# Attention per query block: denominators and values in four 32-column groups, the reciprocal on VectorE, and the first tile's q/k/v between the matmuls of the last layer-0 MLP

## The chip, the cores and the metric

The kernel runs on all eight NeuronCores of one Trainium2 chip, one launch, each core on its own half of one sample. The metric is the device time of the slowest core in microseconds (us). An execution can fall in a slower state, in which the cores of one die get a lower TensorE clock (one of e1_lnexp: 1792.11 us, four cores at 0.816 to 0.822, the other four at 0.983 to 0.991); every run lists the clock and span of each core, and only runs of the fast state are compared here. Engine names in the profile: PE is TensorE (PEld its weight loads), DVE is VectorE, ACT is ScalarE, POOL is GpSimd.

## The reference, cut to what matters

Two layers over 4 samples of 4096 tokens of width 1024, in front of each a modulated RMSNorm, behind each mixer a squared-ReLU MLP. Layer 0 mixes by pooling, layer 1 by windowed attention, which is where the change lies:

```python
# window_attention: 16 heads of 64, 2 key/value heads, blocks of 128 queries
q = rope_2d(q, ang) * qscale;  k = rope_2d(k, ang)
s_win  = ...   # keys of the previous, own and next block, |i-j| <= 128
s_ctx  = ...   # 256 context keys
p = softmax(concat([s_win, s_ctx, s_sink], -1))     # a sink logit per head
o = p_win @ v_win + p_ctx @ v_ctx
y = o.reshape(B, L, 1024) @ w_o
```

For one query block of 128 there are five key blocks of 128: previous, next, own, and two of context. The kernel keeps probabilities transposed (keys on partitions), so a softmax denominator is a matmul with a matrix of ones, and division follows the values.

## The kernel before

Every operation is recorded with the tiles that it reads and writes. A list scheduler then orders each engine's instructions with a cost per instruction that is written in the code, and the order is fixed from then on. All matmuls go through one helper and have one line in the profile (L378; L387 after the change), so groups are told apart by their tiles. A matmul whose weights have 64 columns writes 64 output partitions, and two of them on different halves run side by side: in the trace of before the two of a pair start within 40 ns, and the next pair follows 0.216 us after them.

```python
SB = [P.bk(0, 2), P.bk(2, 2)]            # scores: two pairs of PSUM banks
OB, DB = P.bk(4), P.bk(5)                # values, denominators; banks 6, 7 serve everything else

def emit_s(p, i):                        # scores of one key block and half (8 heads), Exp on ScalarE, mask
    ...
    P.act(pt.rearrange("p a b -> p (a b)"), sb, AF.Exp, scale=0.125)
    ...

def emit_pv(p):                          # p: query block and half
    qb, hf = pairs[p]
    for v in range(2):                   # the sink starts the denominator
        P.mm(DB[64 * v:64 * v + 64, :]..., ONES, ESKR[...], start=True, stop=False)
    for i in (2, 3, 4, 0, 1):
        for v in range(2):
            P.mm(DB[64 * v:64 * v + 64, :], ONES, pt_of(p, i)[:, v, :], start=False, stop=(i == 1))
    for i in (2, 3, 4, 0, 1):
        kb, _ = kbs_of(qb)[i]
        for v in range(2):
            P.mm(OB[64 * v:64 * v + 64, :], VA[:, kb, 64 * v:64 * v + 64], pt_of(p, i)[:, v, :], start=(i == 2), stop=(i == 1))

def emit_o(p):
    ...
    P.act(DN, DB, AF.Ln)                 # 1/x as exp(-ln x), twice over 128x512
    P.act(DN, DN, AF.Exp, scale=-1.0)
    P.tt(QT[...][...], OB..., DN..., ALU.mult)
```

Between scores and values the loop over 80 steps fills in other TensorE work: projections of tiles 1 to 3 (512 tokens each), the output projections, and the first matmuls of the layer-1 MLP. The projections of the 384-column halo and context tile (tile 4) and of tile 0 come before the loop, after the last layer-0 MLP:

```python
spread(mlp_2(gb), wkv_dma + n4 + n0, 4)          # the last MLP half; norms of tiles 4 and 0 between its matmuls
...
run_all(l1_proj(4))
...
spread(l1_proj(0), l1_norm(1, RS[0]), 1)         # k, v, q of tile 0: matmul, then rope on VectorE and GpSimd
```

The softmax here doesn't subtract the row's maximum and nothing guards it: scores larger than these inputs give would overflow.

## Time and profile before

| | before |
|---|---|
| time, median of the first 3 runs | 1549.28 us (1548.54 to 1549.91) |
| spans of the eight cores, profiled run | 1538.8 to 1544.6 us, clock 0.984 to 0.989 |
| TensorE busy | 94% of the span |
| TensorE idle in attention (777 to 1082 us) | 30 us of 305 |

The first part of the page of before (busy us of each engine, share of the span, instructions) and the first line of its chain of waits (who held the chain that ended last):

```profile
PE 1453.5 (94%) x8116; PEld 703.0 (46%) x8116; DVE 604.2 (39%) x1003; ACT 593.9 (38%) x860; POOL 303.0 (20%) x369
...
PE 88%; DVE 3%; DMA 3%; issue 3%; ACT 2%; POOL 1%; SPq 0%; DVEq 0%; ACTq 0%; POOLq 0%
```

TensorE is the bottleneck. What it does less of can count in full; what other engines do counts only where TensorE waits. The windows view of before, over attention (columns: stretch, its length, busy us and instructions of PE, PEld, DVE, ACT and POOL, granted clock, DMA share, GB/s):

```profile
777.00:1082.00 305.00, 274.75 (x1727) 110.77 (x1726) 170.25 (x253) 216.78 (x262) 161.36 (x148) 0.96 0.12 21
```

Here TensorE is idle for 30 us and its clock is cut to 0.96 on average. The clock takes two values in the clock records of before, 1 and 0.5, so 0.96 means 2 x 0.04 x 305, some 24 us at half clock. TensorE's waits of before in attention (who waited for whom, us in total, times, longest):

```profile
PE ps L378 <- POOL qt_115 L405: 6.0, 1, 6.0
PE ps L378 <- DVE tbe_126 L419: 3.5, 1, 3.5
PE ps L378 <- POOL pt_113 L424: 3.4, 1, 3.4
```

The two longest are the start: the first scores wait for tile 0's q, which comes out of a chain of VectorE and GpSimd work. The timeline of TensorE before, one half block (start, length, operation, count):

```profile
1046.04 0.41 PE L378 MATMUL ps<-eskr_50,ones_47 128*64 128x512 bf16 x2
1046.28 0.38 PE L378 MATMUL ps<-pt_108,ones_47 128*64 128x512 bf16 x2
1046.50 0.38 PE L378 MATMUL ps<-pt_109,ones_47 128*64 128x512 bf16 x2
...
1048.22 0.38 PE L378 MATMUL ps<-pt_107,va_105 128*64 128x512 bf16 x2
1048.54 0.61 PE L378 MATMUL ps<-qt_118,kt_104 64*128 64x512 bf16 x4
```

Lengths overlap (0.38 us, while the next pair starts after 0.22 us); the start-to-start distance is what counts. A pair takes one slot of 0.216 us. A half block has eleven slots (one for the sink, five for denominators, five for values), 2.50 us from its first matmul to the next scores.

### The profile page before, as it was taken

Reading aid. Unit: us, or ns where it says so; the run is one execution under the profiler, and the core shown is the slowest. Engines: PE = TensorE matmul, PEld = TensorE weight load, DVE = VectorE, ACT = ScalarE, POOL = GpSimd, SP = SyncE. Lnnn points to the kernel's source line nnn. Section 1 sums busy time; section 2 is a strip of 40 time slices with the busy share of each in tenths; the row PEclk is TensorE's granted clock in tenths of the full one; section 3 lists DMA queues with packets and bytes.
Section 4 is the critical chain, followed back from the end, with each engine's and each line's share of the span. In section 5 each row is a group of like instructions: output and inputs, shape, how many; then the busy total and the mean of one; then the engine's idle time right before and its main releaser. Section 6 shows DMA issues by size and latency. Waiting matters only on the chain.

```text
span 1544.6 us, 22776 instructions; the slowest of 8 cores (1538.8 to 1544.6 us)
## 1 busy us (share of the span) xinstructions
PE 1453.5 (94%) x8116; PEld 703.0 (46%) x8116; DVE 604.2 (39%) x1003; ACT 593.9 (38%) x860; POOL 303.0 (20%) x369
## 2 busy tenths in 40 slices
PE   1699899999999999999978989989999999999996
PEld 0344345555555555555533433333444444444442
DVE  0177874442221444222188664433343221553013
ACT  2464363335110333331047858877234221432001
POOL 2025400101100001000137664444000000000000
PEclk9999999999999999999989989999999999999998
DMA  9554715455653454653340012001244444654432
GB/s 191 147 123 79 127 28 96 83 102 90 113 106 66 85 96 83 112 107 67 63 69 8 8 28 42 0 1 28 42 82 70 78 72 75 129 123 83 71 66 109
DMA packets 38958, 121.69 MB, mean 79 GB/s; under 512 B 3904, under 2 KB 4288, under 8 KB 38464
## 3 DMA queue, kind: packets, MB, share of 16 engines
q0 software_dynamic: 28656, 100.48, 37.8%
q1 hardware_dynamic: 10192, 19.76, 4.0%
q8 instruction: 67, 1.10, 0.3%
q14 instruction: 43, 0.35, 0.1%
HBM read 212.30 MB, written 8.39 MB: 143 GB/s over the span
## 4 chain that ended last, share of the span: by engine, by line
PE 88%; DVE 3%; DMA 3%; issue 3%; ACT 2%; POOL 1%; SPq 0%; DVEq 0%; ACTq 0%; POOLq 0%
PE ps L378 88%; DMA xm_55<-xT 2%; DMA ring_59<-ada_r 0%; DVE xm_55 L415 0%; DMA ring_58<-ada_r 0%; SPq L438 0%; DVE tmp_64 L405 0%; ACT xb_68 L388 0%; DVE tmp_65 L405 0%; ACT rs_63 L388 0%; DVE tb_122 L419 0%; ACT pt_112 L388 0%; DVE tb_121 L405 0%; POOL h_134 L412 0%; DVE tb_123 L405 0%
## 5 line engine op out<-in xcount | busy, mean ns | idle before, releaser
L415 DVE SCALAR_TENSOR_TENSOR xm_55<-ps,mod_44,xm_55 128x512 f32<-128x512 f32 (+2 forms) x136 | 97.4, 719 | 338.4 <-PE ps L378 337.9
L388 ACT ACTIVATE tmp_64<-ps 128x512 f32<-128x512 f32 (+2 forms) x155 | 84.0, 542 | 228.3 <-PE ps L378 176.2
L388 ACT ACTIVATE tmp_65<-ps 128x512 f32<-128x512 f32 (+2 forms) x155 | 84.0, 542 | 141.5 <-PE ps L378 77.0
L388 ACT ACTIVATE sqf_169<-xm_55 128x1024 bf16<-128x1024 f32 x16 | 16.6, 1051 | 158.6 <-DVE xm_55 L415 156.6
L378 PE MATMUL ps<-xb_68,win_67 128*128 128x512 bf16 (+1 forms) x192 | 50.6, 424 | 10.2 <-ACT xb_68 L388 9.5
L378 PE MATMUL ps<-h_0_98,ring_61 128*128 128x408 bf16 (+3 forms) x336 | 58.9, 335 | 0.0
L378 PE MATMUL ps<-h_0_98,ring_58 128*128 128x384 bf16 (+3 forms) x336 | 58.9, 335 | 0.0
L388 ACT ACTIVATE rs_63<-ps,epsv_51 128x512 f32<-128x512 f32 (+3 forms) x16 | 10.6, 664 | 123.6 <-PE ps L378 123.5
L405 DVE TENSOR_TENSOR tmp_64<-xm_55,rs_63 128x512 f32<-128x512 f32 (+2 forms) x44 | 37.4, 850 | 43.7 <-ACT rs_63 L388 35.8
L378 PE MATMUL ps<-h_0_98,ring_60 128*128 128x416 bf16 (+3 forms) x288 | 50.5, 335 | 0.0
L378 PE MATMUL ps<-h_0_98,ring_59 128*128 128x416 bf16 (+3 forms) x288 | 50.4, 334 | 0.0
L378 PE MATMUL ps<-h_0_98,ring_57 128*128 128x416 bf16 (+3 forms) x288 | 50.4, 334 | 0.0
L438 POOL DMA_DIRECT2D ring_61<-w_r x27 | 14.3, 531 | 162.5 <-PE ps L378 162.0
L405 DVE TENSOR_TENSOR hid_100<-tmp_64 128x416 bf16<-128x416 f32 (+3 forms) x48 | 27.9, 581 | 43.1 <-ACT tmp_64 L388 43.1
L438 POOL DMA_DIRECT2D ring_59<-w_r x27 | 14.4, 533 | 151.7 <-PE ps L378 144.5
L378 PEld LDWEIGHTS ps<-h_0_98,ring_61 128*128 128x128 bf16 x336 | 32.5, 97 | 25.1 <-issue 0.6
L405 DVE TENSOR_TENSOR hid_99<-tmp_64 128x416 bf16<-128x416 f32 (+3 forms) x48 | 27.9, 581 | 40.8 <-ACT tmp_64 L388 40.6
L378 PEld LDWEIGHTS ps<-h_0_98,ring_58 128*128 128x128 bf16 x336 | 32.5, 98 | 25.0 <-issue 0.8
L405 DVE TENSOR_TENSOR hid_99<-tmp_65 128x416 bf16<-128x416 f32 (+3 forms) x48 | 27.9, 581 | 38.2 <-ACT tmp_65 L388 38.2
L405 DVE TENSOR_TENSOR hid_100<-tmp_65 128x416 bf16<-128x416 f32 (+3 forms) x48 | 27.9, 581 | 36.8 <-ACT tmp_65 L388 36.8
L378 PE MATMUL ps<-hid_99,ring_61 128*128 128x416 bf16 (+3 forms) x240 | 42.1, 335 | 0.0
L388 ACT ACTIVATE h_134<-xm_55 128x1024 bf16<-128x1024 f32 (+1 forms) x12 | 15.9, 1344 | 67.9 <-PE ps L378 67.9
(769 smaller groups left out, 3083.1 us busy)
## 6 DMA issues: line engine op xcount, KB each, us to landing
ring_61<-w_r POOLq DMA_DIRECT2D x27, 512.0 KB, 5.2
ring_59<-w_r POOLq DMA_DIRECT2D x27, 512.0 KB, 5.7
ring_57<-w_r POOLq DMA_DIRECT2D x25, 512.0 KB, 5.2
ring_58<-w_r POOLq DMA_DIRECT2D x25, 512.0 KB, 5.1
ring_60<-w_r POOLq DMA_DIRECT2D x24, 512.0 KB, 5.1
outT<-xm_55 SPq DMA_DIRECT2D x16, 512.0 KB, 3.3
xm_55<-xT SPq DMA_DIRECT2D x6, 1024.0 KB, 8.7
ring_58<-ada_r POOLq DMA_DIRECT2D x12, 512.0 KB, 6.0
```

What stands on the lines that cost most here:

```text
L378: return self.S.op("pe", lambda e: e.matmul(out, lhsT, rhs, start=start, stop=stop), reads=[lhsT, rhs], writes=[out], cost=max(30.0 if hal ...
L388: return self.S.op("act", lambda e: e.activation(out, in_, func, bias=bias, scale=scale), reads=[in_, scale, bias], writes=[out], cost=175 ...
L405: return self.S.op(eng, lambda e: e.tensor_tensor(out, in0, in1, op), reads=[in0, in1], writes=[out], cost=self.ew_cost(eng, "tt", out, [i ...
L415: return self.S.op("dve", lambda e: e.scalar_tensor_tensor(out, in0, scalar, in1, op0, op1), reads=[in0, in1, scalar], writes=[out], cost= ...
L438: return self.S.op(q, lambda e: e.dma_start(out=out, in_=in_), reads=[in_], writes=[out], chan="dma:" + slot, inc=16, extra_deps=dep, cost ...
```

## The change

The intent has three parts.

1. The 32 denominator-and-value passes, one per half block, become 16, one per query block, with four weight groups of 32 columns side by side. Denominators need only 6 slots a block instead of 12; values stay at 10.
2. The reciprocal of the denominators is taken on VectorE, in place of Ln and Exp on ScalarE.
3. Tile 4's k and v and tile 0's k, v and q are made between the matmuls of the last layer-0 MLP, with the squares and statistics of tiles 1 and 2.

The two banks 4 and 5 now go round: denominators, first value half, second value half, and so on, so the second value half writes the bank from which the reciprocal reads. The diff, cut to its core:

```diff
+    def recip(self, out, in_):
+        return self.S.op("dve", lambda e: e.reciprocal(out, in_), reads=[in_], writes=[out], cost=160.0 + 1.04 * self.n_of(out))
...
-    OB, DB = P.bk(4), P.bk(5)
+    AB = [P.bk(4), P.bk(5)]
...
-    def emit_pv(p): ...
-    def emit_o(p): ...
+    def emit_pv(qb):
+        groups = [(hf, v) for hf in range(2) for v in range(2)]
+        q0 = (qb % 4) * 128
+        db = rot("ab", AB)
+        with S.one():
+            for g in range(4):
+                P.mm(db[32 * g:32 * g + 32, :]..., ONES, ESKR[...], start=True, stop=False)
+            for i in range(5):
+                for g, (hf, v) in enumerate(groups):
+                    P.mm(db[32 * g:32 * g + 32, :], ONES, pt_of(qb, i, hf)[:, v, :], start=False, stop=(i == 4))
+        with S.first(20):
+            P.recip(DN, db)
+        for dh in range(2):
+            ob = rot("ab", AB)
+            with S.one():
+                for i in range(5):
+                    kb, _ = kbs_of(qb)[i]
+                    for g, (hf, v) in enumerate(groups):
+                        P.mm(ob[32 * g:32 * g + 32, :], VA[:, kb, 64 * v + 32 * dh:64 * v + 32 * dh + 32], pt_of(qb, i, hf)[:, v, :],
+                             start=(i == 0), stop=(i == 4))
+            with S.first(20):
+                P.tt(QT[qb // 4][:, 4 * dh:4 * dh + 4, q0:q0 + 128], ob..., DN..., ALU.mult)
...
-    spread(mlp_2(gb), wkv_dma + n4 + n0, 4)
+    sides_gb = n4 + [early_dma] + kv_pieces(4) + n0 + kv_pieces(0)     # q of tile 0 rides on the weight stream
+    for _ in mlp_2(gb):
+        step += 1
+        if sides_gb:
+            sides_gb.pop(0)()
+        if step % 6 == 0 and step >= 18:
+            ...
+            for t in (1, 2):
+                stat_chunk(t, step // 6 - 3)
...                                        # SBUF places, 12 probability tiles, filler 1500 instead of 2500 ns a step,
...                                        # output-projection rows permuted to match
```

More of the change, by code (lines that the diff above doesn't have):

```diff
@@ L161, in f, with first @@
             self.hold, self.boost = None, 0
+        return f()
+    def first(self, boost):
+        @contextmanager
+        def f():
+            self.boost = boost
+            yield
+            self.boost = 0
         return f()
@@ L378, in mm @@
         return self.S.op("pe", lambda e: e.matmul(out, lhsT, rhs, start=start, stop=stop), reads=[lhsT, rhs], writes=[out],
-                         cost=max(30.0 if half else 62.0, (n / 2.4 + 2.5) * (0.5 if half and n > 64 else 1.0)),
+                         cost=max(30.0 if half else 62.0, (n / 2.4 + 2.5) * (min(rows, cols) / 128.0 if n > 64 else 1.0)),
                          mode=(rows, cols), join=join)
@@ L526, in build @@
     ONESM = const("onesm", [128], BF16)
-    ONES = const("ones", [64], BF16)
+    ONES = const("ones", [32], BF16)
     CTF = const("ctf", [16], F32)
@@ L560, in build @@
     ada_n = [0]
+    extra = {}
     def ada_mm(slot, c, MB):
@@ L604, in w_take @@
             pass
+        nxt = ST.items[ST.pos][0]
+        if nxt[0] in extra:
+            extra[nxt[0]](*nxt[1:])
         return ST.take(key)
@@ L611, in build, with plan_mlp @@
             ST0.add(("ada", 0, r, c), d_ada[0, r, c])
-    def plan_mlp(l, g, rounds1, rounds2):
+    def plan_mlp(l, g, rounds1, rounds2, q0={}):
         ext1 = [("ada", l_, r_, c) for l_, r_ in rounds1 for c in range(4)]
@@ L622, in plan_mlp @@
             ST.add(("w2", l, g, j), d_w2[l, j // 2, j % 2])
+            if j in q0:
+                ST.add(("wq0", q0[j]), d_wq[q0[j]])
             if ext2 and j >= 1:
@@ L628, in build @@
     plan_mlp(0, 0, [(0, 5), (1, 1)], [(1, 0), (1, 2)])
-    plan_mlp(0, 1, [(1, 3), (1, 4)], [(1, 5)])
+    plan_mlp(0, 1, [(1, 3), (1, 4)], [(1, 5)], {11: 0, 12: 1, 13: 2, 14: 3})
     for i in range(4):
@@ L652, in norm_sq, with rms_of @@
             o += n
+    def rms_of(bk, N, rs):
+        P.act(rs[:, 0:N], bk[:, 0:N], AF.Ln, bias=EPSV)
+        P.act(rs[:, 0:N], rs[:, 0:N], AF.Exp, scale=-0.5)
     def norm_stat(sq, N, rs):
@@ L657, in norm_stat @@
             P.mm(bk[:, 0:N], ONESM, sq[:, c, 0:N], start=(c == 0), stop=(c == NCH - 1))
-        P.act(rs[:, 0:N], bk[:, 0:N], AF.Ln, bias=EPSV)
-        P.act(rs[:, 0:N], rs[:, 0:N], AF.Exp, scale=-0.5)
+        rms_of(bk, N, rs)
     def norm_apply(tile, rs, l, n, h, c, eng="act", tmps=None):
@@ L1032, in build @@
     DN = P.t("dn", E0 + 9728, [512], F32)
-    PT = [ft("pt", i * 2048, [2, 512], BF16) for i in range(8)]
-    QTO = (16384, 24576, 65536, 73728)
+    ROPE0 = P.t("ropee", E0 + 9728, [1024], BF16)
+    ROPE4 = P.t("ropee", E0 + 11776, [2, 128], BF16)
+    PT = [ft("pt", i * 2048, [2, 512], BF16) for i in range(12)]
+    QTO = (38912, 24576, 74752, 38912)
     QT = [ft("qt", o, [NCH, 512], BF16) for o in QTO]
-    WO0, WO17 = ft("wo", 32768, [1024], BF16), ft("wo", 81920, [7, 1024], BF16)
-    TBO = (34816, 36864, 38912, 40960, 43008)
+    WO0, WO17 = ft("wo", 32768, [1024], BF16), ft("wo", 82944, [7, 1024], BF16)
+    TBO = (34816, 36864, 66560, 68608, 55296)
     TB = [ft("tb", o, [512], F32) for o in TBO[0:4]]
-    TBE = [ft("tbe", i * 2048, [512], F32) for i in range(8)]
-    HB = [ft("h", o, [NCH * 512], BF16) for o in (45056, 57344)]
-    HH = {4: sqv(ft("h", 38912, [NCH * 384], BF16), 384), 0: sqv(HB[0], 512), 1: sqv(HB[1], 512), 2: sqv(HB[0], 512), 3: sqv(HB[1], 512)}
-    WKV = ft("wkv", 53248, [2, NCH, 128], BF16)
+    TB4 = [ft("tbk", 55296 + i * 512, [128], F32) for i in range(2)]
+    TBK = [ft("tbk", o, [512], F32) for o in (43008, 45056)]
+    HB = [ft("h", o, [NCH * 512], BF16) for o in (47104, 58368)]
+    HH = {4: sqv(ft("h", 47104, [NCH * 384], BF16), 384), 0: sqv(HB[0], 512), 1: sqv(HB[1], 512), 2: sqv(HB[0], 512), 3: sqv(HB[1], 512)}
+    WKV0, WKV1 = [ft("wkv", o, [2, NCH, 128], BF16) for o in (38912, 70656)]
     SHUF = [i ^ 16 for i in range(32)]
@@ L1059, in rope_dma, with rope, l1_kv @@
         k = rot("rope", [0, 1])
-        rope_of[t] = rope_slots[k]
-        P.dma("pool", rope_of[t], d_rope[t].rearrange("p a b -> p (a b)"), slot="rope%d" % k)
-    def l1_proj(t):
+        rope_of[t] = rope_slots[k].rearrange("p (a b) -> p a b", a=2)
+        P.dma("pool", rope_slots[k], d_rope[t].rearrange("p a b -> p (a b)"), slot="rope%d" % k)
+    def rope(t, ba, dst, n, tb, post=None):
+        rp = rope_of[t]
+        t1, sh = rot("tb%d" % len(tb), tb)[:, 0:n], rot("tb%d" % len(tb), tb)[:, 0:n]
+        with S.first(10):
+            P.tt(t1, ba[:, 0:n], rp[:, 0, 0:n], ALU.mult)
+            P.shuf(sh, ba[:, 0:n], SHUF)
+        if post is not None:
+            post()
+        P.tt(sh, sh, rp[:, 1, 0:n], ALU.mult, eng="dve")
+        P.tt(dst, t1, sh, ALU.add, eng="pool")
+    def l1_kv(t):
         tile, b0 = tiles[t], b0_of[t]
@@ L1067, in l1_proj @@
         h = HH[t]
-        rp = rope_of[t].rearrange("p (a b) -> p a b", a=2)
+        WKV = WKV0 if t in (0, 4) else WKV1
         R = N if t < 4 else NHALO
-        def rope(ba, dst, n, post=None):
-            early = t in (4, 0)
-            t1 = rot("tb%d" % early, TBE if early else TB)[:, 0:n]
-            sh = rot("tb%d" % early, TBE if early else TB)[:, 0:n]
-            P.tt(t1, ba[:, 0:n], rp[:, 0, 0:n], ALU.mult)
-            P.shuf(sh, ba[:, 0:n], SHUF)
-            if post is not None:
-                post()
-            P.tt(sh, sh, rp[:, 1, 0:n], ALU.mult, eng="dve")
-            P.tt(dst, t1, sh, ALU.add, eng="pool")
         ba = P.bank()
@@ L1090, in post @@
                 P.act(KT[:, 17 * 128:19 * 128], ba[:, NHALO:N], AF.Copy)
-        rope(ba, KT[:, b0 * 128:b0 * 128 + R], R, post)
+        rope(t, ba, KT[:, b0 * 128:b0 * 128 + R], R, TB4 if t == 4 else TBK if t == 0 else TB, post)
         yield 4 * N * MMN
@@ L1100, in l1_proj, with l1_q @@
         P.act(VA[:, b0:b0 + nb, :], bv[:, 0:N].rearrange("p (a b) -> p a b", a=nb), AF.Copy)
-        if t == 4:
-            return
+    def l1_q(t):
         for c in range(NCH):
@@ L1105, in l1_proj, with q0_unit, pt_of, emit_s @@
             for kc in range(NCH):
-                P.mm(ba[:, 0:N], wq_unit(c)[:, kc, :], h[:, kc, :], start=(kc == 0), stop=(kc == NCH - 1))
+                P.mm(ba, wq_unit(c)[:, kc, :], HH[t][:, kc, :], start=(kc == 0), stop=(kc == NCH - 1))
                 if kc == 3:
-                    yield 4 * N * MMN
-            rope(ba, QT[t][:, c, :], N)
-            yield 4 * N * MMN
+                    yield 4 * 512 * MMN
+            rope(t, ba, QT[t][:, c, :], 512, TB)
+            yield 4 * 512 * MMN
+    def q0_unit(i):
+        w = ST.take(("wq0", i)).rearrange("p (u a b) -> p u a b", u=2, a=NCH)
+        ba = P.bank()
+        for u in range(2):
+            for kc in range(NCH):
+                P.mm(ba, w[:, u, kc, :], HH[0][:, kc, :], start=(kc == 0), stop=(kc == NCH - 1))
+            rope(0, ba, QT[0][:, 2 * i + u, :], 512, TMP)
+        ST.free()
+    def l1_proj(t):
+        yield from l1_kv(t)
+        yield from l1_q(t)
     SB = [P.bk(0, 2), P.bk(2, 2)]
-    OB, DB = P.bk(4), P.bk(5)
+    AB = [P.bk(4), P.bk(5)]
     def kbs_of(qb):
         return [(qb - 1 if qb > 0 else 16, "prev"), (qb + 1 if qb < 15 else 16, "next"), (qb, None), (17, None), (18, None)]
-    pairs = [(qb, half_) for qb in range(16) for half_ in range(2)]
-    def pt_of(p, i):
-        return PT[(5 * p + i) % 8]
-    def emit_s(p, i):
-        qb, hf = pairs[p]
+    def pt_of(qb, i, hf):
+        return PT[(10 * qb + 2 * i + hf) % 12]
+    def emit_s(qb, i, hf):
         kb, mk = kbs_of(qb)[i]
@@ L1131, in emit_s @@
             P.mm(sb[:, v * 512:(v + 1) * 512], KT[r, kb * 128:(kb + 1) * 128], qv[r, hf * 4:hf * 4 + 4, q0:q0 + 128])
-        pt = pt_of(p, i)
+        pt = pt_of(qb, i, hf)
         P.act(pt.rearrange("p a b -> p (a b)"), sb, AF.Exp, scale=0.125)
@@ L1141, in emit_s @@
             P.asel(ptv, ptv, [[0, 8], [1, 128]], 0, -1)
-    def emit_pv(p):
-        qb, hf = pairs[p]
-        for v in range(2):
-            P.mm(DB[64 * v:64 * v + 64, :].rearrange("p (a b) -> p a b", a=4), ONES,
-                 ESKR[:, hf * 8 + v * 4:hf * 8 + v * 4 + 4].unsqueeze(2).to_broadcast([128, 4, 128]), start=True, stop=False)
-        for i in (2, 3, 4, 0, 1):
-            for v in range(2):
-                P.mm(DB[64 * v:64 * v + 64, :], ONES, pt_of(p, i)[:, v, :], start=False, stop=(i == 1))
-        for i in (2, 3, 4, 0, 1):
-            kb, _ = kbs_of(qb)[i]
-            for v in range(2):
-                P.mm(OB[64 * v:64 * v + 64, :], VA[:, kb, 64 * v:64 * v + 64], pt_of(p, i)[:, v, :], start=(i == 2), stop=(i == 1))
-    def emit_o(p):
-        qb, hf = pairs[p]
-        P.act(DN, DB, AF.Ln)
-        P.act(DN, DN, AF.Exp, scale=-1.0)
-        q0 = (qb % 4) * 128
-        P.tt(QT[qb // 4][:, hf * 4:hf * 4 + 4, q0:q0 + 128], OB.rearrange("p (a b) -> p a b", a=4),
-             DN.rearrange("p (a b) -> p a b", a=4), ALU.mult)
+    def emit_pv(qb):
+        groups = [(hf, v) for hf in range(2) for v in range(2)]
+        q0 = (qb % 4) * 128
+        db = rot("ab", AB)
+        with S.one():
+            for g in range(4):
+                P.mm(db[32 * g:32 * g + 32, :].rearrange("p (a b) -> p a b", a=4), ONES,
+                     ESKR[:, 4 * g:4 * g + 4].unsqueeze(2).to_broadcast([128, 4, 128]), start=True, stop=False)
+            for i in range(5):
[12 more added lines that the diff above has]
+            with S.first(20):
+                P.tt(QT[qb // 4][:, 4 * dh:4 * dh + 4, q0:q0 + 128], ob.rearrange("p (a b) -> p a b", a=4),
+                     DN.rearrange("p (a b) -> p a b", a=4), ALU.mult)
     def wo_mm(t):
@@ L1173, in wo_mm, with early_dma, kv_pieces, stat_chunk @@
             xv = tiles[t][0][0]
-            P.stt(xv[:, fo, :], bk, MOD[:, 1, 16 + fo, 0:1], xv[:, fo, :], ALU.mult, ALU.add)
+            with S.first(10):
+                P.stt(xv[:, fo, :], bk, MOD[:, 1, 16 + fo, 0:1], xv[:, fo, :], ALU.mult, ALU.add)
             yield 4 * 512 * MMN
     n4, n0 = l1_norm(4, RS[0]), l1_norm(0, RS[1])
-    wkv_dma = [lambda: P.dma("pool", WKV.rearrange("p a b c -> p (a b c)"), d_wkv, slot="wkv")]
-    spread(mlp_2(gb), wkv_dma + n4 + n0, 4)
+    def early_dma():
+        P.dma("pool", WKV0.rearrange("p a b c -> p (a b c)"), d_wkv, slot="wkv")
+        rope_of[4], rope_of[0] = ROPE4, ROPE0.rearrange("p (a b) -> p a b", a=2)
+        P.dma("pool", ROPE4, d_rope[4][:, :, 0:128], slot="ropee0")
+        P.dma("pool", ROPE0, d_rope[0].rearrange("p a b -> p (a b)"), slot="ropee1")
+    def kv_pieces(t):
+        gen = l1_kv(t)
+        n = 2 + width(tiles[t]) // 128
+        return [lambda: next(gen)] * n + [lambda: run_all(gen)]
+    extra["wq0"] = q0_unit
+    SQP = [ft("sqp", 110336 + i * 1024, [512], BF16) for i in range(4)]
+    sides_gb = n4 + [early_dma] + kv_pieces(4) + n0 + kv_pieces(0)
+    def stat_chunk(t, c):
+        sq = rot("sqp", SQP)
+        P.act(sq, XM[:, c, t * 512:(t + 1) * 512], AF.Square)
+        P.mm(P.bk(8 - t), ONESM, sq, start=(c == 0), stop=(c == NCH - 1))
+    step = 0
+    for _ in mlp_2(gb):
[3 more added lines that the diff above has]
+        if step % 6 == 0 and step >= 18:
+            ada_flush()
+            for t in (1, 2):
+                stat_chunk(t, step // 6 - 3)
+    for c in (6, 7):
+        for t in (1, 2):
+            stat_chunk(t, c)
+    for t in (1, 2):
+        rms_of(P.bk(8 - t), 512, RS[t - 1])
+    assert not sides_gb
     ada_flush()
@@ L1185, in build @@
     rope_slots.extend([rs_[:, 0:1024], rs_[:, 1024:2048]])
-    rope_dma(4)
-    rope_dma(0)
+    rope_dma(1)
+    rope_dma(2)
+    P.dma("pool", WKV1.rearrange("p a b c -> p (a b c)"), d_wkv, slot="wkv")
     P.dma("pool", WO17.rearrange("p a b -> p (a b)"), d_wo[:, 1024:8192], slot="wo17")
@@ L1197, in build @@
     P.stt(ESKR, ESH, ROW01[:, 1:2], ESF, ALU.mult, ALU.add)
-    P.ring = list(range(8))
-    P.rr = 3
-    run_all(l1_proj(4))
-    rope_dma(1)
-    spread(l1_proj(0), l1_norm(1, RS[0]), 1)
     P.ring = [6, 7]
@@ L1207, in build @@
     H2L1 = [sqv(HB[0], 512), sqv(HB[1], 512)]
-    HROW = [53248, 55296] + list(TBO) + [o + 2048 * i for o in QTO[0:3] for i in range(4)] + [2048 * i for i in range(8)] + \
+    HROW = [70656, 72704] + list(TBO) + [QTO[t] + 2048 * i for t in (1, 2) for i in range(4)] + [2048 * i for i in range(12)] + \
            [32768] + [QTO[3] + 2048 * i for i in range(4)]
@@ L1218, in build @@
     m0, m1 = st_norm(l1[0], 0, "pool", 4), st_norm(l1[0], 1, "pool", 4)
-    n2, n3 = l1_norm(2, RS[1], "pool", 4), l1_norm(3, RS[0], "pool", 4)
+    n2, n3 = l1_norm(2, RS[1], "pool", 4)[5:], l1_norm(3, RS[0], "pool", 4)
     mlp_a = mlp_1(l1[0], True)
-    p_next, p_wait, o_done = 0, [], [0]
+    o_done = [0]
     done = set()
-    def flush_o():
-        while p_wait:
-            emit_o(p_wait.pop(0))
-            o_done[0] += 1
+    n1 = l1_norm(1, RS[0])[3:]
     def ring_on():
@@ L1232, in ring_on @@
         yield
-    work = [("proj1", lambda: True, l1_proj(1)), ("proj2", lambda: "n2" in done, l1_proj(2)), ("proj3", lambda: "n3" in done, l1_proj(3)),
-            ("ring", lambda: True, ring_on()), ("wo0", lambda: o_done[0] >= 8, wo_mm(0)), ("wo1", lambda: o_done[0] >= 16, wo_mm(1)),
-            ("wo2", lambda: o_done[0] >= 24, wo_mm(2)), ("mlp", lambda: "m0" in done and "m1" in done, mlp_a)]
-    sides = [("n2", lambda: True, n2), ("n3", lambda: "proj1" in done, n3), ("m0", lambda: "wo0" in done, m0), ("m1", lambda: "wo1" in done, m1)]
+    work = [("proj1", lambda: "n1" in done, l1_proj(1)), ("proj2", lambda: "n2" in done, l1_proj(2)), ("wo0", lambda: o_done[0] >= 4, wo_mm(0)),
+            ("proj3", lambda: "n3" in done, l1_proj(3)), ("ring", lambda: True, ring_on()),
+            ("wo1", lambda: o_done[0] >= 8, wo_mm(1)), ("wo2", lambda: o_done[0] >= 12, wo_mm(2)),
+            ("mlp", lambda: "m0" in done and "m1" in done, mlp_a)]
+    sides = [("n2", lambda: "n1" in done, n2), ("n3", lambda: "proj1" in done, n3), ("m0", lambda: "proj2" in done and "wo0" in done, m0),
+             ("m1", lambda: "proj3" in done and "wo1" in done, m1)]
     def step_work():
@@ L1265, in step_side @@
                 done.add(sides.pop(0)[0])
-    rope_of_t = {"proj1": 2, "proj2": 3}
-    roped = set()
-    F_NS = 2500.0
     for k in range(80):
-        if 2 * k + 1 >= 30 and (2 * k + 1 - 30) // 40 < 3:
-            finish("proj%d" % ((2 * k + 1 - 30) // 40 + 1))
+        qb, i = k // 5, k % 5
+        if k in (15, 35, 55):
+            finish("proj%d" % (k // 20 + 1))
         with S.one():
-            for s in (2 * k, 2 * k + 1):
-                emit_s(s // 5, s % 5)
-        flush_o()
-        if 5 * p_next + 4 <= 2 * k - 1:
-            with S.one():
-                emit_pv(p_next)
-            p_wait.append(p_next)
-            p_next += 1
-        else:
-            fill(F_NS)
-        step_side()
-        for nm, t in rope_of_t.items():
-            if nm in done and t not in roped:
-                roped.add(t)
-                rope_dma(t)
-    while p_next < 32:
-        emit_pv(p_next)
-        p_wait.append(p_next)
-        p_next += 1
+            for hf in range(2):
+                emit_s(qb, i, hf)
+        if k > 0 and i == 0:
+            emit_pv(qb - 1)
+            o_done[0] += 1
+        else:
+            fill(1500.0)
+        if k < 3:
+            for _ in range(4):
+                if n1:
+                    n1.pop(0)()
+            if not n1:
+                done.add("n1")
+        step_side()
+        if "proj1" in done and 3 not in rope_of:
+            rope_dma(3)
     finish("wo2")
-    flush_o()
+    emit_pv(15)
     while sides:
@@ L1388, in _shared_weights @@
     sh["wkv_r"] = np.concatenate([_wl(wqkv[:, 1152:1280]), _wl(wqkv[:, 1024:1152])], axis=1)
-    sh["wo_r"] = _wl(np.asarray(inp["attn_w_o"], f)[0][qcols, :])
+    wo_perm = qcols.reshape(2, 4, 2, 2, 32).transpose(3, 1, 0, 2, 4).reshape(-1)
+    sh["wo_r"] = _wl(np.asarray(inp["attn_w_o"], f)[0][wo_perm, :])
     sh["ident"] = np.eye(128, dtype=f)
```

## The prediction

> **What bounds it now.** TensorE. On the page it is busy 94% of the 1544.6 us span and holds 88% of the chain of waits; all cores run alike (clock about 0.99). The exception is attention: windows over 777 to 1082 us show TensorE busy 274.8 of 305 us, so some 30 us idle, while ScalarE is busy 217, VectorE 170 and GpSimd 161 us. The waits there: 6.0 us for the first tile's q (made on the GpSimd after a VectorE chain), 3.5 us for a bank read by that chain's shuffle, 3.4 us for a mask, the rest many of about 1 us. Granted clock falls to 0.63 at 800-810 and 890-900 us, worth a few us.
>
> **What the change removes.** In the timeline a 64-column pair of matmuls takes one 0.216 us slot. One half block (11 slots) takes 2.50 us; 22 slots per query block. With four 32-column groups: sinks 1, denominators 5, values 10, so 16 slots. Six slots x 16 blocks x 0.216 = 20.7 us, all TensorE, so all critical; half the mode changes (about 0.1 us each) add 1 to 2 us. Does four-way work at full rate? The modulation matmuls already use 128x32 weights: eight of 256 columns take 0.33 us, mode change included, so yes here. [...]
> ScalarE loses Ln and Exp of the denominators: 32 x (0.60 + 0.63) = 39.5 us, mostly off the critical path.
>
> **What it moves.** K/v of the halo tile and k/v/q of tile 0 (about 20 us of TensorE), and the statistics of tiles 1 and 2, go into the last layer-0 MLP, where VectorE is only 13-20% busy: same TensorE work, but the 10 us idle at 790-805 and most of the cold clock go.
>
> **What it adds.** 16 reciprocals of 128x512 from PSUM. The kernel's scheduler assumes 0.69 us, like other 128x512 PSUM reads. [...] The second value half reuses the denominator's bank, so it waits for the reciprocal; only the first half's 5 slots (1.08 us) cover it. At 3 to 4 us that is about 2.2 to 3.2 us idle per block, 35 to 50 us in all: the gain handed back.
>
> **Sum.** 1549 - 22 (slots) - about 34 (old idle and cold clock) + about 15 (remaining idle) = 1508 with a fast reciprocal; + 35 to 45 = about 1548 with a slow one. Slow gets 65%: 1535 us, range 1500 to 1559. Chances: faster 0.36, same 0.59, slower 0.05.
>
> **What would show it.** Quad slots of 0.216 us; block of 16 slots about 3.6 us if unbroken. The reciprocal's mean ns: 690 or 3000+. Waits of TensorE on the reciprocal's output 16 times, 2 to 3 us each. Idle before the first scores near zero. ScalarE busy down 40 us. The MLP stage longer by about 24 us, still fully busy.
>
> **What would make it wrong.** A four-way slot slower at 512 columns; ScalarE's exponentials (2.05 us per two, against about 2.35 us of TensorE per step) becoming the pace; PE stalls inside the MLP from the shared bank of each q pair.

Two passages that were taken from outside this case's traces and runs are cut out of the record; the cuts are marked. The time of a reciprocal, the "3 to 4 us", and with it the "+ 35 to 45", was the author's assumption (measured afterwards: 3353 ns, 16 waits, 43.7 us). The sum came to 1508 us with a fast reciprocal and to about 1548 us with a slow one, and 35% of the one with 65% of the other to about 1535. "Mode change" stands for the step from the pairs to matmuls of another shape: in before the last pair is followed by the next scores after 0.32 us (1048.22 to 1048.54), 0.10 us more than a slot.

## The result, and the profile after

| | before | after |
|---|---|---|
| median, 4 runs each | 1548.91 us | 1572.30 us (1571.28 to 1573.92) |
| ratio to before | | 1.0152 (95% interval 1.0134 to 1.0170) |
| spans of the cores, profiled run | 1538.8 to 1544.6 us | 1561.9 to 1569.7 us |
| clock of the cores over the whole span | 0.984 to 0.989 | 0.969 to 0.981 |

A ratio here is the mean time of one kernel's fast runs over that of the other's fast runs of the same rounds, so it is not quite the ratio of the medians. The change is slower by 1.5%, 23 us. All cores show it alike.

The page of after, the same two lines, then the chain's second line and the reciprocal's line among the costliest groups (busy us, mean ns, then idle before it):

```profile
PE 1445.0 (92%) x8436; PEld 695.7 (44%) x8436; DVE 648.9 (41%) x1019; ACT 564.4 (36%) x809; POOL 299.9 (19%) x371
...
PE 86%; DVE 6%; DMA 4%; issue 2%; ACT 1%; POOL 0%; SPq 0%; DVEq 0%; ACTq 0%; POOLq 0%
PE ps L387 85%; DVE dn_106 L428 3%; DMA xm_55<-xT 2%; DMA ring_58<-ada_r 1%; ACT rs_63 L397 0%; DMA ring_59<-ada_r 0%; DVE xm_55 L424 0%; DVE tb_129 L414 0%; SPq L450 0%; DVE tmp_65 L414 0%; DVE tb_127 L414 0%; DVE tb_130 L431 0%; ACT xb_68 L397 0%; DVE tmp_64 L414 0%; DVE tb_128 L431 0%
...
L428 DVE RECIPROCAL dn_106<-ps 128x512 f32<-128x512 f32 x16 | 53.6, 3353 | 15.9 <-PE ps L387 15.9
```

The reciprocal takes 3353 ns, not the 692 that the scheduler was told, and it is now a member of the chain that ended last. TensorE's waits after, in attention:

```profile
PE ps L387 <- DVE dn_106 L428: 43.7, 16, 3.6
PE ps L387 <- ACT pt_112 L397: 5.4, 2, 4.9
PE ps L387 <- ACT pt_109 L397: 4.5, 2, 3.5
PE ps L387 <- DVE tb_128 L431: 2.4, 1, 2.4
```

Sixteen waits on the reciprocal's result, one a block, 43.7 us in all, more than all the idle time in attention before. One of them, in the timeline of after:

```profile
1043.38 0.40 PE L387 MATMUL ps<-eskr_50,ones_47 128*32 128x512 bf16 x4
1043.61 0.38 PE L387 MATMUL ps<-pt_109,ones_47 128*32 128x512 bf16 x2
1043.61 0.38 PE L387 MATMUL ps<-pt_110,ones_47 128*32 128x512 bf16 x2
1043.82 0.38 PE L387 MATMUL ps<-pt_111,ones_47 128*32 128x512 bf16 x2
...
1044.98 3.36 DVE L428 RECIPROCAL dn_106<-ps 128x512 f32<-128x512 f32 x1
...
1045.55 0.38 PE L387 MATMUL ps<-pt_118,va_105 128*32 128x512 bf16 x2
...
1048.48 0.39 PE L387 MATMUL ps<-pt_109,va_105 128*32 128x512 bf16 x2 [2.55 <-DVE dn_106 L428]
```

Four matmuls (two lines of x2 with the same start) now share one slot of 0.21 us, so the four-way groups do what they should. But the first value half ends at about 1045.9 us, the reciprocal runs until 1048.34, and the second half cannot write the bank before that: 2.55 us of idle TensorE.

There is a second cost. The windows of after: first the stretch in which attention lies, then four slices of 10 us (columns as above; the clock is the third number from the end):

```profile
768.00:1115.00 347.00, 285.74 (x2136) 113.31 (x2135) 212.32 (x263) 182.56 (x200) 152.00 (x146) 0.92 0.15 26
930.00:940.00 10.00, 7.45 (x72) 2.46 (x64) 5.00 (x4) 5.10 (x7) 3.49 (x4) 0.83 0.01 2
1040.00:1050.00 10.00, 7.45 (x86) 2.94 (x84) 8.19 (x9) 4.09 (x5) 5.51 (x6) 1.00 0.00 0
1060.00:1070.00 10.00, 7.45 (x85) 2.98 (x78) 5.65 (x5) 4.67 (x6) 5.44 (x6) 1.00 0.01 2
1080.00:1090.00 10.00, 8.04 (x48) 2.60 (x48) 5.08 (x7) 4.79 (x5) 1.36 (x2) 0.83 0.01 2
```

For the same stretch the clock of before is 0.97. Adding up the trace's clock records between 640 and 1115 us, TensorE is at half clock for 20.9 us before and 53.3 us after (means of eight cores), in 2.4 and 11.6 pieces. The pieces are multiples of 3.4 us (on the slowest core of after, records of 3413 to 13653 ns): a slice of 10 us at 0.83 holds one of them.

The traces kept say more. On each core of after, the starts and ends of all pieces in attention lie on one grid of 3413 ns, to about 1 ns. Cut by that grid, the attention of after (768 to 1115 us, eight cores) has 681 cells at full clock. In 80 of them the profile shows TensorE busy for less than 40% of the cell, and the next cell was at half clock every time; in 526 it was busy for over 56%, and the next was at half clock not once; of the 75 between, 13 were followed by one. The same stretch of before gives 16 of 16 and 0 of 717. The attention of all twelve traces together gives 242 of 244 and 0 of 8350 (the two exceptions are in e9_copytrue, whose trace lacks 1% of its matmuls). So a cell followed by half clock was not always idle throughout, and a wait shorter than 3413 ns was followed by half clock or not by where it fell on the grid. On the core shown, the wait that ends at 1081.2 us left its cell 32% busy and was followed by a piece at half clock; those that end at 1048.5 and 1064.9 us, equally long, left theirs 50% busy and more and were not.

In that piece a slot takes 0.43 us (1081.54 to 1081.97 us) in place of 0.216, so the 32.4 us more at half clock cost at most half of that, an estimate of 16 us. Part of the waits is thus paid twice, once idle and once as slow matmuls afterwards.

### The profile page after: what moved, and what is told of

It is laid out like the page before. It is cut to its first block, busy times and chain, and to the rows that moved or that the text cites. A ratio compares the mean times of both kernels' runs of the same rounds, so it can differ in the third digit from the quotient of the medians.

```text
span 1569.7 us, 23285 instructions; the slowest of 8 cores (1561.9 to 1569.7 us)
## 1 busy us (share of the span) xinstructions
PE 1445.0 (92%) x8436; PEld 695.7 (44%) x8436; DVE 648.9 (41%) x1019; ACT 564.4 (36%) x809; POOL 299.9 (19%) x371
## 4 chain that ended last, share of the span: by engine, by line
PE 86%; DVE 6%; DMA 4%; issue 2%; ACT 1%; POOL 0%; SPq 0%; DVEq 0%; ACTq 0%; POOLq 0%
PE ps L387 85%; DVE dn_106 L428 3%; DMA xm_55<-xT 2%; DMA ring_58<-ada_r 1%; ACT rs_63 L397 0%; DMA ring_59<-ada_r 0%; DVE xm_55 L424 0%; DVE tb_129 L414 0%; SPq L450 0%; DVE tmp_65 L414 0%; DVE tb_127 L414 0%; DVE tb_130 L431 0%; ACT xb_68 L397 0%; DVE tmp_64 L414 0%; DVE tb_128 L431 0%
## 5 line engine op out<-in xcount | busy, mean ns | idle before, releaser
L428 DVE RECIPROCAL dn_106<-ps 128x512 f32<-128x512 f32 x16 | 53.6, 3353 | 15.9 <-PE ps L387 15.9
L414 DVE TENSOR_TENSOR tmp_64<-xm_55,rs_63 128x512 f32<-128x512 f32 (+2 forms) x44 | 33.1, 753 | 47.3 <-ACT rs_63 L397 41.0
L387 PE MATMUL ps<-hid_99,ring_61 128*128 128x416 bf16 (+3 forms) x288 | 51.0, 335 | 0.0
L387 PE MATMUL ps<-h_0_98,ring_60 128*128 128x416 bf16 (+3 forms) x288 | 50.5, 335 | 0.0
L387 PE MATMUL ps<-h_0_98,ring_59 128*128 128x416 bf16 (+3 forms) x288 | 50.5, 335 | 0.0
L387 PE MATMUL ps<-h_0_98,ring_57 128*128 128x416 bf16 (+3 forms) x288 | 50.4, 335 | 0.0
L387 PEld LDWEIGHTS ps<-h_0_98,ring_58 128*128 128x128 bf16 x336 | 32.4, 98 | 25.0 <-issue 0.8
```

Of the source, the lines that this page charges most:

```text
L387: return self.S.op("pe", lambda e: e.matmul(out, lhsT, rhs, start=start, stop=stop), reads=[lhsT, rhs], writes=[out], cost=max(30.0 if hal ...
L414: return self.S.op(eng, lambda e: e.tensor_tensor(out, in0, in1, op), reads=[in0, in1], writes=[out], cost=self.ew_cost(eng, "tt", out, [i ...
L428: return self.S.op("dve", lambda e: e.reciprocal(out, in_), reads=[in_], writes=[out], cost=160.0 + 1.04 * self.n_of(out))
```

## The experiments

Theories, before the runs. R: the reciprocal's 3.35 us holds the bank that the second value half needs. O: it is VectorE's extra 53.6 us of work as such, with ropes, residuals and norms queueing behind it. M: the moved first-tile work or the new start of attention costs the time. Q: the four-way groups are not as fast as they look. C, beside R: a good part of the loss is the half clock after each wait. Every kernel below gave correct results. Executions in which one die ran at a lower clock are left out of the means. Before was run in the same rounds each time (medians 1547.4 to 1547.9 us).

| run | median of its fast runs, us | ratio to before | 95% interval |
|---|---|---|---|
| the change | 1572.3 | 1.0152 | 1.0134 to 1.0170 |
| e1_lnexp | 1515.6 | 0.9797 | 0.9781 to 0.9814 |
| e2_truecost | 1539.7 | 0.9952 | 0.9935 to 0.9968 |
| e3_copyfirst | 1529.9 | 0.9890 | 0.9874 to 0.9907 |
| e4_warm | 1559.4 | 1.0074 | 1.0057 to 1.0091 |
| e5_unmove | 1560.8 | 1.0077 | 1.0048 to 1.0107 |
| e6_pairs | 1533.8 | 0.9902 | 0.9881 to 0.9923 |
| e7_occupy | 1524.7 | 0.9845 | 0.9818 to 0.9871 |
| e8_start | 1513.9 | 0.9775 | 0.9756 to 0.9793 |
| e9_copytrue | 1524.9 | 0.9847 | 0.9829 to 0.9865 |
| e10_sizes | 1516.8 (one run) | | |

Differences in us below are differences of these ratios times 1548 us, so each kernel is held against before of its own rounds.

### e1_lnexp: the reciprocal back to ScalarE, all else kept

```diff
-            P.recip(DN, db)
+            P.act(DN, db, AF.Ln)
+            P.act(DN, DN, AF.Exp, scale=-1.0)
```

> The changed kernel with the 16 reciprocals replaced by Ln and Exp(-x) on ScalarE over the same 128x512 tile; the four 32-column groups, the moved projections and everything else stay. Theory R (the reciprocal's 3.35 us on VectorE holds the bank that the second value half needs; TensorE waits 43.7 us and then runs part of the time at half clock): about 1516 us, 1506 to 1526; no TensorE wait on the denominators above 1 us; mean clock back to about 0.985. Rival M (the moved first-tile work, or the start of attention, costs the time): 1555 us or more. Rival Q (four-way groups are slower than pairs): also 1555 or more.

Measured: 0.9797, 31 us faster than before and 55 us faster than the change. TensorE's waits in attention, of e1:

```profile
PE ps L387 <- ACT pt L397: 14.5, 11, 4.9
PE ps L387 <- DVE tb L431: 5.3, 5, 2.4
PE ps L387 <- issue: 2.5, 16, 0.2
```

No wait on the denominators is left (Ln and Exp of the tile take 603 and 629 ns, medians of e1, against 3353 for the reciprocal), and half-clock time is 19.6 us, as before the change. Rivals M and Q fall as the main cause: with the move and the groups in place the kernel is well ahead of before. (Some 1% of this trace's matmul records are missing: 8350 matmuls against 8436 weight loads.)

### e2_truecost: only the scheduler's knowledge

```diff
-        ... cost=160.0 + 1.04 * self.n_of(out))
+        ... cost=3350.0)
```

> The changed kernel; only the scheduler's cost of a reciprocal goes from 692 to 3350 ns, so that it may put other matmuls between the two value halves. Same instructions. Theory R with the wait at the bank as the cause: TensorE's wait on the reciprocal falls from 43.7 to under 15 us and the time to 1520 to 1540 us. Rival O (VectorE being occupied for 53.6 us is itself the cost: ropes, residuals and norms queue behind it): stays at 1555 us or more.

Measured: 0.9952, 31 us faster than the change with the same operations. The waits on the reciprocal shrink from 43.7 to 13.0 us (15 waits), half-clock time from 53.3 to 28.6 us:

```profile
PE ps L387 <- ACT pt L397: 21.9, 27, 4.9
PE ps L387 <- DVE dn L428: 13.0, 15, 2.3
PE ps L387 <- DVE tb L431: 2.2, 4, 1.1
```

So over half of the loss was a wrong number in a cost model: the order was fixed for a reciprocal that fits behind the first value half. Rival O, which asks for 1555 us or more, falls as the main cause.

### e3_copyfirst: free the bank, keep VectorE as busy

```diff
-            P.recip(DN, db)
+            P.act(DN, db, AF.Copy)
+            P.recip(DN, DN)
```

> The changed kernel; ScalarE copies the denominators out of the bank (about 0.6 us) and VectorE takes the reciprocal in place in SBUF, with the scheduler's cost left at 692 ns. The bank is free after the copy, VectorE is as occupied as before. Theory R (bank): the 16 waits on the reciprocal go, 1520 to 1540 us, what is left being the two multiplies that wait for it. Rival O (occupied VectorE): 1555 us or more.

Measured: 0.9890, 41 us faster than the change, although the 16 reciprocals in SBUF take as long (median 3352 ns) and the cost told to the scheduler is still 692 ns. TensorE waits for no reciprocal any more (first line: the reciprocals in the tile view of e3, shortest/median/longest ns; then the waits):

```profile
L428 DVE RECIPROCAL dn<-dn x16: 3337/3352/3354, 823.9 to 1051.1; 128x512 f32<-128x512 f32 x16
...
PE ps L387 <- ACT pt L397: 14.2, 11, 4.9
PE ps L387 <- DVE tb L431: 10.9, 6, 3.0
PE ps L387 <- DVE qt L414: 5.0, 2, 3.0
PE ps L387 <- DVE xm L424: 2.1, 3, 1.3
```

This is the bank shown directly: the wait was for the bank's release, not for the quotient. What is left against e1, 14 us, shows mainly as waits for rope banks (tb: 10.9 us against 5.3) and for products (qt: 5.0 against 0.4).

### e4_warm: useless matmuls inside the wait

```diff
-                for i in range(5):
+                for i in list(range(5)) * (3 if dh == 0 else 1):
```

> The changed kernel; the first value half is computed three times over into the same bank (each time from start, so the result is the same), 16 x 10 slots x 0.216 us = 34.5 us of useless matmuls, most of them inside the wait for the reciprocal. Theory C (a good part of the loss is the half clock after each wait): waits on the reciprocal fall to about 10 us, half-clock time in attention falls from some 55 us to under 25 us, and the time falls to 1553 to 1566 us although TensorE does more. Rival W (only the waits count, the clock hardly): 1571 to 1576 us.

Measured: 1.0074, 12 us faster than the change, although its trace holds 555 more matmul records (640 were added; some records are missing). The waits on the reciprocal fall to 12.8 us, that is by 30.9, while an estimated 34.5 us of useless slots (160 x 0.216) are added; by waits and work alone the kernel should have got 3.6 us slower. Half-clock time falls from 53.3 to 15.8 us. The estimate that follows is about 16 us of the change's loss for the clock; half of the 37.5 us, at most 19, agrees. It is an estimate: another order goes with the extra work, although the other waits hardly differ (13.7 us on the probabilities, 3.1 on rope banks). Theory C holds in direction; rival W's 1571 to 1576 us is clearly missed. The waits of e4 and its stretch of attention, in two views:

```profile
PE ps L387 <- ACT pt L397: 13.7, 11, 4.9
PE ps L387 <- DVE dn L428: 12.8, 15, 2.3
```

```profile
768.00:1115.00 347.00, 313.17 (x2805) 133.77 (x2829) 216.39 (x269) 186.91 (x208) 156.21 (x148) 0.97 0.17 29
```

The clock over the stretch is back at 0.97.

### e5_unmove: the move undone, which was not a clean undo

```diff
 (on e1_lnexp)
...                                        # tile 0's q weights come after the MLP's in the stream
-        if sides_gb:
-            sides_gb.pop(0)()
...
-    assert not sides_gb
+    for f in sides_gb:
+        f()
...
+    for i in range(4):
+        q0_unit(i)
```

> e1_lnexp (denominators by Ln and Exp on ScalarE) with the move undone: norms, k, v and q of the halo tile and of tile 0 come after the last layer-0 MLP instead of between its matmuls. So this is the four-way groups without the move. Prediction's account: the move is worth the 10 us idle and part of the half clock of before, so 1525 to 1540 us here against e1's 1517. Rival (the move is worth nothing once VectorE is free): within 4 us of e1.

Measured: 1.0077, far outside the expectation (two fast runs). The reason is mine: the change had packed these pieces for a place where nothing hurries, with two scratch tiles for tile 0's ropes, where before had eight. The squares and statistics of tiles 1 and 2 stay in the MLP. Run bare, the chain is exposed: TensorE waits for norm pieces (h) and ropes (tmp), and 62.7 us are at half clock (mean of eight cores):

```profile
PE ps L387 <- ACT h L397: 19.6, 14, 3.4
PE ps L387 <- DVE tmp L431: 15.8, 4, 5.7
```

So this run says that these pieces need other work around them, not what the move is worth. The next one does.

### e6_pairs: the four-way groups undone

On e1, `emit_pv` with the 64-column pairs, Ln and Exp of before; the move and the loop stay.

```diff
 (on e1_lnexp)
-        db = rot("ab", AB)
-        ... four groups of 32 columns, one Ln and Exp, two value halves
+        for hf in range(2):
+            db, ob = rot("ab", AB), rot("ab", AB)
+            ... pairs of 64 columns: sink, five denominators, five values; Ln, Exp, multiply
...                                        # ones of 64 columns, output-projection rows as before
```

> e1_lnexp with the four-way groups undone: denominators and values as 64-column pairs, 22 slots a query block in place of 16, the move kept, Ln and Exp per half block as before. Prediction's account: 96 slots x 0.216 = 20.7 us more TensorE work, all of it seen: 1536 to 1543 us. Rival (four-way gains little because something else paces attention): below 1528 us.

Measured: 0.9902. Against before that is all but the groups, the move with its new loop, places and order: 15 us. Against e1 it is the groups: 16 us, four short of the slot count of 20.7, and the time lies a little under the stated range. (ScalarE also makes 32 pairs of Ln and Exp here in place of 16.) TensorE's waits in attention, of e6:

```profile
PE ps L387 <- ACT pt L397: 15.0, 13, 4.8
PE ps L387 <- DVE tb L431: 1.7, 1, 1.7
```

The slots do take 0.21 us each, so part of the freed time is spent elsewhere: all waits of the traced core sum to 18.0 us here and 23.4 in e1, rope banks (tb) 1.7 against 5.3, and half-clock time is 15.4 us against 19.6 (means of eight cores). That would account for the four, but it rests on one profile of each. Rival Q's "below 1528" is missed.

### e7_occupy: VectorE busy, nobody waiting

```diff
 (on e1_lnexp, after the block's two multiplies)
+        P.recip(DN, DN)
```

> e1_lnexp plus 16 reciprocals of 128x512 in SBUF whose results nobody uses, each after the block's two multiplies: VectorE is occupied for another 53.6 us, no matmul and no multiply waits for a result. If occupation alone is cheap (theory R): 1518 to 1530 us, at most what e3_copyfirst showed (1530). If it is what costs (rival O): 1545 us or more.

Measured: 0.9845, 7 us over e1. That is the price of 53.6 us more on an engine that is off the chain: rope banks are freed later (11.1 us of waits against 5.3):

```profile
PE ps L387 <- DVE tb L431: 11.1, 6, 3.1
```

Rival O's 1545 us is missed by 20.

### e8_start: the start of attention

After the change the first scores come as soon as the MLP ends, but then TensorE is nearly idle. The window of after:

```profile
794.00:805.00 11.00, 2.54 (x9) 0.50 (x7) 6.55 (x12) 9.27 (x14) 1.87 (x3) 0.66 1.02 157
```

ScalarE (9.27 of 11 us) has squares, two rms, exponentials and the scale-and-shift of tile 1 in its queue.

```diff
 (on e1_lnexp)
-    for t in (1, 2):
-        rms_of(P.bk(8 - t), 512, RS[t - 1])
+    rms_of(P.bk(7), 512, RS[0])
...
-    n1 = l1_norm(1, RS[0])[3:]
+    n1 = l1_norm(1, RS[0], "pool")[3:]
+    n1.insert(4, lambda: rms_of(P.bk(6), 512, RS[1]))
```

> e1_lnexp with the start of attention relieved: tile 1's eight scale-and-shift pieces go from ScalarE to GpSimd, and the rms of tile 2 is taken after the first score blocks instead of before. If the 8.5 us idle and the 13.7 us of half clock at the start are ScalarE's queue: 1506 to 1514 us. If the start is bound by the statistics themselves: within 2 us of e1 (1517).

Measured: 0.9775 (four fast runs, 1512.87 to 1515.04 us), the fastest of all: 2.25% under before, 3.7% under the change by the two ratios. The longest wait on a probability tile falls from 4.9 to 2.2 us, and all of these waits from 14.5 to 10.8:

```profile
PE ps L387 <- ACT pt L397: 10.8, 19, 2.2
```

The intervals of e8 and e1 overlap, and by the medians of their fast runs (1513.9 and 1515.6) the two are within 2 us, so the gain of 2 to 3 us is likely, not certain. The expectation does not separate its two cases at this size: 1513.9 lies in the first range and also within 2 us of e1.

### e9_copytrue: the best form found with the reciprocal on VectorE

e3's copy and e2's cost together.

```diff
-            P.recip(DN, db)
+            P.act(DN, db, AF.Copy)
+            P.recip(DN, DN)
...
-        ... cost=160.0 + 1.04 * self.n_of(out))
+        ... cost=3350.0)
```

> e3_copyfirst (copy to SBUF, reciprocal there) with the scheduler told 3350 ns for the reciprocal: the best form I know that keeps the reciprocal on VectorE. If what e3 still lost against e1 (1530 against 1517) was queueing that a right cost avoids: 1518 to 1525 us. If it is plain occupation of VectorE (e7_occupy: 1525): 1524 to 1530.

Measured: 0.9847, the same as e7, where the reciprocals are mere ballast. Both parts of the expectation allow it. Bank and order are thus mended, and the 8 us left to e1 are what occupation alone costs in e7, 7 us. That the two have the same cause is argued from the size, not shown: e9's waits are spread otherwise (rope banks 4.9 us, products 5.4, residuals 4.8).

### e10_sizes: the size law

On e1, unused reciprocals of 256 and of 64 columns in each block.

```diff
 (on e1_lnexp, after the block's two multiplies)
+        P.recip(DN[:, 0:256], DN[:, 0:256])
+        P.recip(DN[:, 256:320], DN[:, 256:320])
```

> e1_lnexp plus, per block, unused reciprocals of 256 and of 64 columns in SBUF, for the size law alone. The 512-column one took 3353 ns. If the cost is a number of VectorE cycles per element and a small fixed part: about 1.7 us at 256 and 0.45 to 0.5 us at 64. If a fixed part dominates: nearer 3 us at 256.

Measured (groups view of e10: busy us, mean ns, idle before):

```profile
L428 DVE RECIPROCAL dn<-dn 128x256 f32<-128x256 f32 x16 | 28.1, 1753 | 1.6
L428 DVE RECIPROCAL dn<-dn 128x64 f32<-128x64 f32 x16 | 7.9, 494 | 0.0
```

With 3353 ns at 512 columns, 256 more cost 1600 ns, 6.25 ns each, in line with the first case of the expectation as to time; how many cycles an element takes was not shown. An estimate from the two sizes leaves some 150 ns fixed (3353 less 512 x 6.25). The 64-column one fits less well: the same slope leaves it 94 ns. A PSUM multiply of 512 columns took 692 ns (after).

## Why the prediction was right or wrong

The prediction named the mechanism and still missed the number: 1572 us lies outside its 1500 to 1559.

Right:

- The groups: "Quad slots of 0.216 us". The trace shows 0.21, and e6 against e1 gives 16 us of gain for the 20.7 counted; "so all critical" was a little too much.
- The reciprocal's wait: "The second value half reuses the denominator's bank, so it waits for the reciprocal". "Waits of TensorE on the reciprocal's output 16 times, 2 to 3 us each" came as 16 times, 43.7 us, 2.7 us each (1.3 to 3.6), inside "35 to 50 us in all". e3 shows that it is the bank. The size had some luck: the "3 to 4 us" for a reciprocal was the author's assumption, not worked out from a trace, and the 3.35 us measured falls inside.
- The move in the MLP: TensorE stays busy there (128.00 of 128 us from 640 to 768 us in the windows of after), and its last matmuls end 22 us later than before (792 against 770 us), for "about 24 us".
- "Idle before the first scores near zero": by the letter, yes. In the timeline of after they start at 793.2 us, right after the MLP.

Wrong, in order of size:

- The step that failed is the term "+ 35 to 45" for a slow reciprocal in "Sum". It counts the waits as idle time and nothing else. Measured (the change against e1) it is 55 us. Left out was the clock. The prediction said "most of the cold clock go"; instead half-clock time rose from 20.9 to 53.3 us: many of the waits, 1.3 to 3.6 us long, left a cell of the 3413 ns grid busy for under 40%, and half clock followed every such cell (80 of 80 in after). e4 puts the clock at about 16 us, an estimate. The traces give nearly the same sum: TensorE's waits of every kind (640 to 1130 us, one core each) are 60.8 us after and 23.4 in e1, 37 apart, inside the predicted 35 to 45; half of the difference in half-clock time (53.3 less 19.6) is 17; together 54, an estimate. Taken instead as a path of measured steps, the 55 us are, rounded: 41 by freeing the bank, waits and clock together (e3), 7 by telling the scheduler the cost (e9 against e3), 8 by relieving VectorE (e1 against e9). Occupation of VectorE, which the prediction did not count either, costs 7 us by itself (e7); it shows once the bank is free.
- The fast sum, 1508, was 8 us too low: e1 measures 1515.6. Groups and move were put at 22 and 19 us (34 of old idle and cold clock less 15 left) and measured 16 and 15.
- "the 10 us idle at 790-805 and most of the cold clock go": the idle time did not go, it moved behind the first scores. TensorE was busy 2.54 of 11 us from 794 to 805 us, with the clock at 0.66. The prediction's 15 us of remaining idle covered it in the sum; e8 recovers about 3 us by the ratios.
- "1535 us" was an average of two cases, neither of which it describes. The slow case alone gave "about 1548". Of the 24 us missing from it, 8 are the fast sum's and some 16 the clock's; the range's upper end, 1559, left room for 11.
- "ScalarE busy down 40 us": it fell by 29.5 us (593.9 to 564.4), although the 32 Ln and Exp pairs (39.5 us) did go. Summed by instruction it fell by 36.0; the busy figure counts overlapping instructions once. The squares of tiles 1 and 2, cut into smaller pieces, took 2 more.

What stays open: the exact share of the clock in the 55 us, since no run changes the clock and nothing else; what decides for cells that are 40% to 56% busy, of which 13 of 75 in after were followed by half clock; and, beyond single profiles, where the four missing microseconds of the groups went.

## What to carry to other kernels

An instruction that is off the busiest engine can still sit on the chain, through the buffer that it reads: ask of each new reader of a PSUM bank how long it holds the bank and which matmul writes there next, and free the bank with a short copy, or take another route, if the reader is slow. Measure a new instruction once before giving its cost to a scheduler; here one wrong cost was worth 31 us while the reciprocal held the bank (7 us once it did not), more than the 16 us that the new matmul groups gained. Count a repeated TensorE wait such as the 2.5 to 3.6 us ones here at more than its length, since matmuls after it may run at half clock (in the attention of before and after always, 96 times of 96, where a cell of the 3413 ns grid was busy for less than 40%), and undo a mixed change part by part: two of its three parts were worth 15 and 16 us, and the third cost 55.
